# The first norm of a decoder block from the transposed x, by halves of the tokens

## The chip, the cores and the metric

The kernel runs on one core of one Trainium2 chip. A core has a matrix engine (TensorE, PE in the profile; its weight loads are shown apart as PEld), three engines for elementwise work (VectorE or DVE, ScalarE or ACT, GpSimd or POOL), and SyncE (SP), whose queue issues most of the transfers. The transfers of all queues run on the same 16 DMA engines. Each engine works through its own instructions in order and waits on semaphores for the others. The metric is the device time of one execution in microseconds (us).

## The reference

One block of a decoder on x of 1024 tokens by 1024 features, in float32, with a conditioning vector c:

```python
mod = jax.nn.silu(c) @ w_ada[l] + b_ada[l]
sh1, sc1, g1, sh2, sc2, g2 = jnp.split(mod, 6, axis=-1)
h = modulate(rms_norm(x, norm1_g[l]), sh1, sc1)
x = x + g1[:, None, :] * token_mixer(h, w_in[l], ...)
h = modulate(rms_norm(x, norm2_g[l]), sh2, sc2)
x = x + g2[:, None, :] * squared_relu_mlp(h, w_ff1[l], w_ff2[l])
...
return rms_norm(x, norm_f_g)
```

`rms_norm` divides each token by the root of the mean of its squares and multiplies by a gain; `modulate(h, shift, scale)` is h (1 + scale) + shift, with one shift and one scale per feature. The token mixer begins with projections of h by `w_in`; the first that the kernel computes is that of the values of one attention head group (`w_av`). Only the first norm, the first modulation and this first projection matter here.

## The kernel before

Features lie on the 128 partitions, tokens along the free dimension: the transposed x is eight tiles `xt[k]` of 128 features by 1024 tokens, and h is kept as a high part `hh[k]` and a low part `hl[k]`, whose sum has nearly float32's precision. Likewise each weight tile is split into a high part (a cast on ScalarE) and a low part (a subtraction on VectorE), and a product is three matmuls: high by high, low by high, high by low.

`startup` (L392) is the head of the program, written out in order by hand. It issues the loads on SP: c, then x by tokens (eight tiles `xn`, with small tables between them), then for each k the two rows of tiles of `w_ada` that make the scale and the shift of feature slice k (`early_load`, L349) and `xt[k]`, with the first weights (`issue`, L77) in between. Buffers of the size of such a tile come from one pool of 26.

c is spread over all partitions by a matmul with a row of ones, and silu of it is kept in `cb` (L417). ScalarE squares the tiles `xn` and adds up each row as it goes (L419), so that `ss1` holds the sums of squares of all tokens, tokens on partitions. `rstd_of` (L367) makes the reciprocal root: one VectorE instruction, then a power of -1/2 on GpSimd. `rstd_bcast` (L373) spreads the result over all partitions, tokens along the free dimension, by matmuls with an identity; 512 tokens make one half.

A scale or a shift of slice k is the product of silu(c) with 128 columns of `w_ada`. `mod1` (L448) computes it on VectorE: one instruction multiplies a 128 x 1024 tile with `cb` and adds up each row. `h1_mods` (L466) adds the biases and makes the gain `a1`. `h1_scale` (L472) multiplies `xt[k]` by gain and reciprocal root on VectorE, and ScalarE adds the shift and writes `hh[k]`. `h1_low` (L480) writes `hl[k]` on VectorE.

The projection is computed slice by slice of h: `av_first` (L867) has one step for two slices. For slice k its body first prepares slice k+1 (biases, scaling, the low half of a weight if one is due, `hl`, the modulation of slice k+2) and then `av_k` (L840) issues 24 matmuls of 512 columns on slice k, three for each of eight blocks of 128 tokens, which add up in eight PSUM banks. Step 0 starts in `startup`, where slice 0 is scaled by halves. `split_first` (L858) casts a weight tile and puts its low half on a list, `first["lows"]`, from which the bodies take it.

What follows (the other projections, retention, attention, the MLP) is the same in both kernels.

Of the kernel before, what the change touches and what calls it, by code (L numbers as in the profile page):

```python
# [17 lines left out]
P = 128  # L18
# [4 lines left out]
C = 128  # L23
# [110 lines left out]
def block_kernel(ctx, tc, io, stop=None, dbg=None):  # L134
# [214 lines left out]
    def early_load(k):  # L349

        for i in (SC1 + k, SH1 + k):
            early[i] = x4(f"em{i}")
            nc.sync.dma_start(early[i], io["w_ada"][i])
        nc.sync.dma_start(xt[k], io["xT"][k])
# [30 lines left out]
    ss1 = xpool.tile([P, NK], F32, name="ss1")  # L385
# [6 lines left out]
    def startup(issue, prepare, limits):  # L392
# [7 lines left out]
        xn = [x4(f"xn{b}") for b in range(NC)]  # L400
        for b in range(NC):
            nc.sync.dma_start(xn[b], io["x"][b])
            if b == 1:
                nc.sync.dma_start(rel[:32], io["rel_bias"])
                for g in range(3):
                    nc.sync.dma_start(bias_cut(onehot, g)[:33], io["onehot"][:, 384 * g:384 * g + 384])
            if b == 4:
                nc.sync.dma_start(ct, io["cst"])
                nc.sync.dma_start(vec, io["vec"])
# [8 lines left out]
        for b in range(NC):  # L418
            nc.scalar.activation(xn[b], xn[b], AF.Square, accum_out=ss1[:, b:b + 1])  # L419
# [12 lines left out]
        first["lows"].pop(0)()  # L432
        mod1(1, (SH1,))

    def bias_rows(g):

        ps = ps_s(f"pb{g}")[:12, :384]
        nc.tensor.matmul(ps, rel[:33], bias_cut(onehot, g)[:33], start=True, stop=True)
        r = bias_cut(rows, g)[:12]
        nc.scalar.copy(r, ps)  # L440
# [25 lines left out]
    def h1_mods(k):  # L466
        sh = mods[:, SH1 + k:SH1 + k + 1]
        nc.vector.tensor_add(sh, sh, vec[:, VC_BADA + SH1 + k:VC_BADA + SH1 + k + 1])
        nc.vector.scalar_tensor_tensor(a1[:, k:k + 1], mods[:, SC1 + k:SC1 + k + 1], bs1[:, k:k + 1],
                                       vec[:, VC_N1 + k:VC_N1 + k + 1], op0=ALU.add, op1=ALU.mult)  # L470

    def h1_scale(k, j=None):  # L472

        ts = slice(0, S) if j is None else slice(512 * j, 512 * j + 512)
# [5 lines left out]
    def h1_low(k):  # L480
        nc.vector.scalar_tensor_tensor(hl[k], xt[k], mods[:, SH1 + k:SH1 + k + 1], fv(hh[k]),
# [352 lines left out]
    def av_k(g, k, w):  # L834

        ws = slice((k % 2) * 512, (k % 2) * 512 + 512)
        if k == 0:
            av[g] = [ps_s(f"av{g}{c}") for c in range(NC)]
        if g == 0:

            parts = ((hh, 0), (hl, 0), (hh, 1)) if k == 0 else ((hh, 1), (hh, 0), (hl, 0))
            groups = (parts[:1], parts[1:2], parts[2:]) if k == 0 else (parts[:2], parts[2:])
        else:
            parts = ((hh, 1), (hh, 0), (hl, 0))
            groups = (parts,)
        for group in groups:
            for c in range(NC):
                for x, j in group:
                    nc.tensor.matmul(av[g][c], x[k][:, c * C:(c + 1) * C], w[j][:, ws], start=k == 0 and (x, j) == parts[0],
# [7 lines left out]

    def split_first(raw):  # L858
        hi = whl.tile([P, 1024], F32R, tag="wh", name=raw.name + "h")
        lo = whl.tile([P, 1024], F32R, tag="wl", name=raw.name + "l")  # L860
        nc.scalar.copy(hi, raw)
        first["lows"].append(lambda: nc.vector.tensor_sub(lo, raw, fv(hi)))
# [1840 lines left out]
```

## Time and profile before

| | us |
|---|---|
| median of 3 runs | 2194.77 (2193.68 to 2197.47) |
| time of the profiled execution | 2196.09 |
| its span | 2194.1 |
| TensorE busy | 2151.7 (98%) |
| VectorE busy | 1472.7 (67%) |
| ScalarE busy | 944.5 (43%) |
| first matmul of the first projection | 23.14 after the span's start |

The profile is one execution. Its span runs from the first instruction to the last; the time of the same execution is 2.0 us longer. In rows of single instructions the first number is the start in us, the second the duration, then come the engine, the line of the code, the operation, output and inputs by the program's names with their shapes, and in brackets how long the engine had been idle before it and what ended that. TensorE's records overlap: a matmul of 512 columns has a duration of 0.39 us, and the next one starts 0.22 to 0.23 us after it, so spacing counts and not duration.

### The profile page before, as it was taken

The numbers are of one execution on the slowest core, as the hardware profiler recorded it, in microseconds if no ns is written. First come the engines' busy times: TensorE is split into PE (matmuls) and PEld (weight loads), VectorE is DVE, ScalarE is ACT, GpSimd is POOL, SyncE is SP. The second block draws the span as 40 slices with busy tenths as digits, with TensorE's granted clock in tenths as the row PEclk, the third lists the DMA queues.
The fourth block names the chain that finished last, engine by engine and source line by source line (L and its number), as shares of the span: only waits on it lengthen the run. The fifth ranks groups of instructions, "written<-read, shape, count | busy, mean of one in ns | idle before, by whom it ended". The sixth has DMA issues, their size and how long they took to land.

```text
span 2194.1 us, 26997 instructions
## 1 busy us (share of the span) xinstructions
PE 2151.7 (98%) x10034; PEld 1784.1 (81%) x10034; DVE 1472.7 (67%) x2271; ACT 944.5 (43%) x1709; POOL 166.4 (8%) x176
## 2 busy tenths in 40 slices
PE   7999999999999999999999999999999999999998
PEld 5888888888888888888788788888878888788887
DVE  6756777767566677755555644777876665787855
ACT  4532322333334566654544524434454544533412
POOL 0101111100001233200000000001000000000003
PEclk9999999999999999999999999999999999999999
DMA  9869999734687745579523364654154435645322
GB/s 382 227 199 293 289 308 279 222 130 149 244 294 291 250 159 192 173 239 258 151 78 107 106 240 170 234 187 139 44 206 149 152 137 193 243 135 175 113 86 78
DMA packets 159906, 422.54 MB, mean 193 GB/s; under 512 B 27478, under 2 KB 55389, under 8 KB 155358
## 3 DMA queue, kind: packets, MB, share of 16 engines
q1 hardware_dynamic: 151902, 372.57, 48.2%
q0 software_dynamic: 7872, 48.24, 9.5%
q8 instruction: 79, 1.29, 0.2%
q14 instruction: 53, 0.43, 0.1%
HBM read 325.71 MB, written 160.32 MB: 222 GB/s over the span
## 4 chain that ended last, share of the span: by engine, by line
PE 84%; DVE 7%; ACT 4%; DMA 3%; issue 1%; SPq 0%; POOL 0%; POOLq 0%; DVEq 0%; ACTq 0%
PE qap L200 6%; PE qap L204 6%; PE qap L202 6%; PE fp L200 4%; PE fp L202 4%; PE fp L204 4%; PE f2a L202 2%; PE f2a L204 2%; PE f2a L200 2%; PE ak L200 1%; PE ak L202 1%; PE ak L204 1%; PE rg L202 1%; PE rg L200 1%; PE rg L204 1%; PE va L204 1%
## 5 line engine op out<-in xcount | busy, mean ns | idle before, releaser
L200 PE MATMUL qap<-hh,qaw 128*128 128x512 f32 x264 | 102.9, 390 | 0.5 <-DVE qat L291 0.5
L204 PE MATMUL qap<-hh,qaw 128*128 128x512 f32 x264 | 102.7, 389 | 0.0
L202 PE MATMUL qap<-hl,qaw 128*128 128x512 f32 x264 | 102.7, 389 | 0.0
L639 POOL TENSOR_TENSOR j<-qk,j 128x512 fp32r<-128x512 f32 x32 | 48.1, 1506 | 324.1 <-ACT j L638 324.1
L2158 ACT ACTIVATE a<-a 128x512 f32<-128x512 f32 x48 | 30.3, 632 | 78.2 <-DVE a L2157 78.2
L2054 POOL TENSOR_TENSOR accnf<-accnf,sqnf 128x256 f32<-128x256 f32 (+1 forms) x18 | 16.6, 922 | 612.4 <-ACT sqnf L2053 612.4
L1510 ACT ACTIVATE P<-P,ng 128x128 f32<-128x128 f32 (+1 forms) x96 | 41.9, 438 | 43.9 <-DVE ng L1507 43.9
L200 PEld LDWEIGHTS qap<-hh,qaw 128*128 128x128 f32 x264 | 49.5, 188 | 11.5 <-DVE qat L291 1.4
L204 PEld LDWEIGHTS qap<-hh,qaw 128*128 128x128 f32 x264 | 49.6, 188 | 10.3
L202 PEld LDWEIGHTS qap<-hl,qaw 128*128 128x128 f32 x264 | 49.5, 188 | 10.3
L2347 ACT CAST w2h<-w2s 128x512 fp32r<-128x512 f32 x36 | 22.4, 621 | 78.4 <-DVE w2s L2385 78.4
L257 DVE TENSOR_TENSOR fw<-w1r,fw 128x512 fp32r<-128x512 f32 x48 | 32.8, 688 | 33.3 <-ACT fw L247 33.3
L257 DVE TENSOR_TENSOR qaw<-wa,qaw 128x512 fp32r<-128x512 f32 x66 | 45.0, 686 | 12.7 <-ACT qaw L247 12.6
L2054 POOL TENSOR_TENSOR accn<-accn,sqn 128x512 f32<-128x512 f32 x12 | 15.5, 1295 | 477.2 <-ACT sqn L2053 477.2
L247 ACT CAST qaw<-wa 128x512 fp32r<-128x512 f32 x66 | 39.8, 617 | 25.5 <-PE qap L204 15.3
L200 PE MATMUL fp<-h2h,fw 128*128 128x512 f32 x128 | 50.0, 391 | 0.0
L204 PE MATMUL fp<-h2h,fw 128*128 128x512 f32 x128 | 49.8, 389 | 0.0
L202 PE MATMUL fp<-h2l,fw 128*128 128x512 f32 x128 | 49.8, 389 | 0.0
L200 PE MATMUL roa<-rh,rwl 128*128 128x512 f32 x128 | 49.8, 389 | 0.0
L202 PE MATMUL roa<-rl,rwh 128*128 128x512 f32 x128 | 49.8, 389 | 0.0
L204 PE MATMUL roa<-rh,rwh 128*128 128x512 f32 x128 | 49.8, 389 | 0.0
L1288 DVE SCALAR_TENSOR_TENSOR cossin<-cossin,cb 128x1024 f32<-128x1024 f32 x32 | 39.0, 1219 | 15.9 <-DMA cossin<-in_w_ada_dram 15.9
(3057 smaller groups left out, 7106.1 us busy)
## 6 DMA issues: line engine op xcount, KB each, us to landing
cossin<-in_w_ada_dram SPq DMA_DIRECT2D x32, 512.0 KB, 5.4
v<-vd SPq DMA_DIRECT2D x32, 512.0 KB, 4.7
w1r<-in_w_ff_dram SPq DMA_DIRECT2D x32, 512.0 KB, 4.9
vd<-vo SPq DMA_DIRECT2D x24, 512.0 KB, 6.6
yt<-y POOLq DMA_DIRECT2D x6, 2048.0 KB, 15.3
xsd<-as SPq DMA_DIRECT2D x24, 512.0 KB, 3.0
w2r<-in_w_ff2s_dram SPq DMA_DIRECT2D x24, 512.0 KB, 7.4
em<-in_w_ada_dram SPq DMA_DIRECT2D x16, 512.0 KB, 10.2
```

The source lines that it names most:

```text
L200: nc.tensor.matmul(o, wl, xh, start=first, stop=False, skip_group_check=skip)
L202: nc.tensor.matmul(o, wh, xl, start=False, stop=False, skip_group_check=skip)
L204: nc.tensor.matmul(o, wh, xh, start=False, stop=last, skip_group_check=skip)
L247: nc.scalar.copy(t[:, :512], src)
L257: nc.vector.tensor_sub(t[:, 512:], src, fv(t[:, :512]))
L639: nc.gpsimd.tensor_sub(t[:, 1], src, fv(t[:, 0]))
L1288: nc.vector.scalar_tensor_tensor(t, t, 1.0, cb, op0=ALU.mult, op1=ALU.mult, accum_out=mods[:, j:j + 1])
L1510: nc.scalar.activation(v, v, AF.Exp, bias=ng[:, blk:blk + 1], accum_out=st[:, g, blk, 2 + a:3 + a])
L2054: (nc.vector if f == 7 else nc.gpsimd).tensor_add(G["acc", key], G["acc", key], sq)
L2158: nc.scalar.activation(o, o, AF.Relu)
L2347: nc.scalar.copy(hi, src)
```

## The change

x by tokens is no longer loaded, nor is `xn` kept. The transposed x is loaded by halves of 512 tokens: after c, the small tables and the scale tile of slice 0, first the eight first halves, then the shift tile of slice 0 and the first weights, then the eight second halves. The tiles of `w_ada` of the slices 1 to 7 follow.

The sums of squares come from the transposed x. For each half, ScalarE squares the eight tiles (`x_square`), VectorE adds them in pairs, and for each pair TensorE takes 128 tokens at a time as weights against a column of ones (`x_sum`), so that the sums of 128 features and of all pairs add up in PSUM, tokens on partitions. Reciprocal root and broadcast are made for each half by itself. One call of the power on GpSimd on other data is put early.

Scale and shift of slice 1 are computed by TensorE (`mod_rows`): eight accumulating matmuls for each, with a 128 x 128 block of the tile as weights and a column of silu(c) as the moving operand. For that the two tiles are stored in another order on the host, and c is loaded once more by columns (`ccol`). One VectorE instruction copies the two resulting columns from PSUM to `mods`.

Slice 0 is worked through by halves of the tokens in `av_start`: three groups of four matmuls for the first half, with the sums of the second half between them, then `mod_rows` and the second broadcast, then the second half. Its weight is split in halves too. The body of slice 0 then scales slice 1, casts the next weight and takes the second low half; the lower half of that next weight is taken one slice later than before.

```diff
-        nc.sync.dma_start(xt[k], io["xT"][k])
+    def xt_load(k, j):
+        hs = slice(512 * j, 512 * j + 512)
+        nc.sync.dma_start(xt[k][:, hs], io["xT"][k][:, hs])
...
-        xn = [x4(f"xn{b}") for b in range(NC)]
-        for b in range(NC):
-            nc.sync.dma_start(xn[b], io["x"][b])
...
-        for k in range(NK):
-            early_load(k)
-            if k in (0, 1, 3):
-                issue((k + 3) // 2)
+        for t, src in ((ccol, "ccol"), (ct, "cst"), (vec, "vec"), (rel[:32], "rel_bias")):
+            nc.sync.dma_start(t, io[src])
+        for g in range(3):
+            nc.sync.dma_start(bias_cut(onehot, g)[:33], io["onehot"][:, 384 * g:384 * g + 384])
+        first["sq"] = [x4(f"n1sq{i}") for i in range(NK // 2)]
+        early_load(0, (SC1,))
+        for k in range(NK):
+            xt_load(k, 0)
+        early_load(0, (SH1,))
+        issue(1)
+        for k in range(NK):
+            xt_load(k, 1)
...
-        for b in range(NC):
-            nc.scalar.activation(xn[b], xn[b], AF.Square, accum_out=ss1[:, b:b + 1])
-        for g in range(3):
-            bias_rows(g)
-        rs = rstd_of(ss1, "n1", xpool)
-        mod1(0)
+        nc.scalar.activation(ccol, ccol, AF.Silu)
+        mod1(0, (SC1,))
+        pb = [ps_s(f"pb{g}")[:12, :384] for g in range(3)]
+        for g in range(3):
+            nc.tensor.matmul(pb[g], rel[:33], bias_cut(onehot, g)[:33], start=True, stop=True)
+        warm = xpool.tile([P, NK], F32, name="warm")
+        nc.gpsimd.tensor_tensor(warm, ones.to_broadcast([P, NK]), mhalf, op=ALU.pow)
+        for k in range(NK):
+            x_square(k, 0)
+            if k % 2:
+                x_sum(k // 2, 0)
         nc.vector.tensor_scalar_add(bs1, vec[:, VC_BADA + SC1:VC_BADA + SC1 + NK], 1.0)
-        h1_mods(0)
-        first["rb"] = [rstd_bcast(rs, 4 * j, 4, f"n1{j}") for j in range(2)]
+        h1_a(0)
+        rs = rstd_of(first["ss", 0], "n1", xpool)
+        for g in range(3):
+            nc.scalar.copy(bias_cut(rows, g)[:12], pb[g])
         prepare(1)
-        for j in range(2):
-            h1_scale(0, j)
-        mod1(1, (SC1,))
-        h1_low(0)
-        first["lows"].pop(0)()
-        mod1(1, (SH1,))
+        first["rb"] = [rstd_bcast(rs, 0, 4, "n10")]
+        mod1(0, (SH1,))
+        h1_sh(0)
+        for k in range(4):
+            x_square(k, 1)
+        h1_scale(0, 0)
+        x_sum(0, 1)
+        h1_low(0, 0)
+        for k in range(1, NK):
+            early_load(k)
+            if k in (2, 4):
+                issue(k // 2 + 1)
+
+    def x_square(k, j):
+        nc.scalar.activation(first["sq"][k // 2][:, 512 * (k % 2):512 * (k % 2) + 512],
+                             xt[k][:, 512 * j:512 * j + 512], AF.Square)
+
+    def x_sum(i, j):
+        t = first["sq"][i]
+        nc.vector.tensor_add(t[:, :512], t[:, :512], t[:, 512:])
+        if i == 0:
+            first["ss", j] = ps_s(f"n1{j}ss")[:, :4]
+        for b in range(4):
+            nc.tensor.matmul(first["ss", j][:, b:b + 1], t[:, b * P:b * P + P], ones, start=i == b == 0,
+                             stop=i == NK // 2 - 1, skip_group_check=True)
+
+    def mod_rows(i, col):
+        for j in range(NK):
+            nc.tensor.matmul(first["md"][:, col:col + 1], early[i][:, j * P:j * P + P], ccol[:, j:j + 1],
+                             start=j == 0, stop=j == NK - 1)
...
         if k == 0:
-            av[g] = [ps_s(f"av{g}{c}") for c in range(NC)]
...
+            return av_start(g, w)
...
+    def av_start(g, w):
+        av[g] = []
...
+        part(0, hh, 0)
+        for k in range(4, NK):
+            x_square(k, 1)
+        x_sum(1, 1)
+        part(0, hl, 0)
+        first["lows"].pop(0)()
+        x_sum(2, 1)
+        part(0, hh, 1)
+        x_sum(3, 1)
+        rs = rstd_of(first["ss", 1], "n1", xpool)
+        first["md"] = ps_s("md")
+        mod_rows(SC1 + 1, 1)
+        first["rb"].append(rstd_bcast(rs, 0, 4, "n11"))
+        mod_rows(SH1 + 1, 0)
+        for j, rb in enumerate(first["rb"]):
+            nc.scalar.copy(rb1[:, 512 * j:512 * j + 512], rb)
+        h1_scale(0, 1)
+        nc.vector.tensor_copy(mods[:, SH1:SH1 + 2 * NK].rearrange("p (a b) -> p a b", b=NK)[:, :, 1], first["md"][:, :2])
+        h1_mods(1)
+        h1_low(0, 1)
+        for x, j in ((hh, 0), (hl, 0), (hh, 1)):
+            part(1, x, j)
...
                 if k == 0:
-                    for j, rb in enumerate(first["rb"]):
-                        nc.scalar.copy(rb1[:, 512 * j:512 * j + 512], rb)
-                if k % 2 == 0:
+                    av_k(0, k, w)
+                elif k % 2 == 0:
                     ahead(1)
                 if k + 1 < NK:
-                    h1_mods(k + 1)
+                    if k > 0:
+                        h1_mods(k + 1)
                     h1_scale(k + 1)
+                    if k == 0:
+                        ahead(1)
...
-                av_k(0, k, w)
+                if k > 0:
+                    av_k(0, k, w)
```

`part(half, x, j)` issues four matmuls, one for each of four blocks of 128 tokens of that half, with part x of slice 0 as weights and part j of `w_av`'s tile as the moving operand.

More of the change, by code (lines that the diff above doesn't have):

```diff
@@ L837, in av_k @@
         if k == 0:
[L838 to L846 removed]
+            return av_start(g, w)
+        parts = ((hh, 1), (hh, 0), (hl, 0))
+        for group in (parts[:2], parts[2:]):
             for c in range(NC):
                 for x, j in group:
[L849 removed]
+                    nc.tensor.matmul(av[g][c], x[k][:, c * C:(c + 1) * C], w[j][:, ws], start=False,
                                      stop=k == NK - 1 and (x, j) == parts[2], skip_group_check=True)
@@ L860, in split_first @@
         lo = whl.tile([P, 1024], F32R, tag="wl", name=raw.name + "l")
-        nc.scalar.copy(hi, raw)
-        first["lows"].append(lambda: nc.vector.tensor_sub(lo, raw, fv(hi)))
+        for j in (None,) if "split" in first else (0, 1):
+            ts = half(j)
+            nc.scalar.copy(hi[:, ts], raw[:, ts])
+            first["lows"].append(lambda ts=ts: nc.vector.tensor_sub(lo[:, ts], raw[:, ts], fv(hi[:, ts])))
+        first["split"] = True
         return hi, lo
```

46 lines of the change are left out of this document (26 added, 20 removed).

## The prediction

> **What bounds the kernel now.** I read the page first, then the busy time by stretches, then the instructions in order of time for the first 45 us, then single lines of the code. The page has TensorE (PE) busy for nearly the whole span:
>
> ```profile
> span 2194.1 us, 26997 instructions
> PE 2151.7 (98%) x10034; PEld 1784.1 (81%) x10034; DVE 1472.7 (67%) x2271; ACT 944.5 (43%) x1709; POOL 166.4 (8%) x176
> ```
>
> So only a stretch in which TensorE has gaps can be worth anything. In the view by stretches (columns: length, then busy us of PE, PEld, DVE, ACT and POOL with counts, then clock, DMA share, GB/s) the gaps lie at the front, and the last two rows split the run at 61.5 us:
>
> ```profile
> 14.00:23.10 9.10, 3.62 (x16) 3.49 (x16) 3.66 (x9) 5.27 (x9) 2.59 (x1) 1.00 1.03 411
> 31.60:38.00 6.40, 5.77 (x24) 4.42 (x24) 6.27 (x10) 1.17 (x2) 0.00 (x0) 1.00 1.03 410
> 45.00:51.00 6.00, 5.44 (x24) 4.20 (x23) 5.86 (x11) 1.15 (x1) 0.00 (x0) 1.00 1.03 410
> 57.00:63.00 6.00, 5.48 (x25) 4.21 (x23) 5.86 (x11) 1.15 (x1) 1.08 (x1) 1.00 1.07 339
> 61.50:2194.10 2132.60, 2105.02 (x9864) 1751.78 (x9864) 1431.52 (x2205) 918.70 (x1673) 162.23 (x170) 1.00 0.57 187
> ```
>
> Before 23.1 us TensorE has done almost nothing that counts. From 31.6 to 63 us VectorE (DVE) is busy for 5.86 of 6.00 us while TensorE has small gaps: there VectorE prepares one of the eight slices of h after the other, and TensorE follows. After 61.5 us TensorE is busy 2105.0 of 2132.6 us, so a delay of the slices goes one to one into the end. The question is when slice 3 can be scaled, since from there the two kernels run the same instructions. Before, the scalings of slices 1, 2 and 3 start at 29.08, 35.51 and 40.80:
>
> ```profile
> 29.08 1.28 DVE L476 SCALAR_TENSOR_TENSOR xt<-xt,a,rb 128x1024 f32<-128x1024 f32 x1
> 30.28 1.22 DVE L862 TENSOR_TENSOR raw_308l<-raw,raw_308h 128x1024 fp32r<-128x1024 f32 x1
> 31.58 1.28 DVE L481 SCALAR_TENSOR_TENSOR hl<-xt,mods,hh 128x1024 fp32r<-128x1024 f32 x1
> 35.51 1.29 DVE L476 SCALAR_TENSOR_TENSOR xt<-xt,a,rb 128x1024 f32<-128x1024 f32 x1
> 40.80 1.29 DVE L476 SCALAR_TENSOR_TENSOR xt<-xt,a,rb 128x1024 f32<-128x1024 f32 x1
> ```
>
> The first step is longer (6.43 us) than the second (5.29 us), because it holds one lower half of a weight (L862) that the second has not.
>
> The start before the change is one chain. The last square of x by tokens (ACT L419) starts at 15.40, then DVE, POOL (the power -1/2), the broadcast on TensorE, the scaling, the first slice's high part, the first matmul at 23.14:
>
> ```profile
> 15.40 1.06 ACT L419 ACTIVATE xn<-xn 128x1024 f32<-128x1024 f32 x1
> 16.58 0.17 DVE L370 TENSOR_SCALAR n1rs<-ss 128x8 f32<-128x8 f32 x1 [15.48 <-ACT xn L419]
> 16.84 2.59 POOL L371 TENSOR_TENSOR n1rs<-n1rs,ct 128x8 f32<-128x8 f32 x1 [16.39 <-DVE n1rs L370]
> 19.48 2.08 PE L378 MATMUL n10rb<-ct,n1rs 128*128 128x128 f32 x8 [8.38 <-POOL n1rs L371]
> 21.59 0.75 DVE L476 SCALAR_TENSOR_TENSOR xt<-xt,a,n10rb 128x512 f32<-128x512 f32 x1 [2.04 <-PE n10rb L378]
> 22.37 0.72 ACT L478 ACTIVATE hh<-xt,mods 128x512 fp32r<-128x512 f32 x1 [0.79 <-DVE xt L476]
> 23.14 1.35 PEld L849 LDWEIGHTS av<-raw_301h,hh 128*128 128x128 f32 x4 [0.18 <-ACT hh L478]
> 26.43 1.69 PEld L849 LDWEIGHTS av<-raw_301h,hl 128*128 128x128 f32 x8 [0.44 <-DVE hl L481]
> 28.17 1.77 PEld L849 LDWEIGHTS av<-raw_301l,hh 128*128 128x128 f32 x8
> ```
>
> **The change part by part. Loads.** Loads of 512 KB follow each other every 1.28 us: the SP rows of three loads are 3.84 us apart,
>
> ```profile
> 0.74 0.35 SPq L398 DMA_DIRECT2D crow<-in_c_dram  x1
> 1.15 0.83 SPq L402 DMA_DIRECT2D xn<-in_x_dram  x2
> 11.15 1.06 ACT L419 ACTIVATE xn<-xn 128x1024 f32<-128x1024 f32 x1 [0.16 <-DMA xn<-in_x_dram]
> 19.25 0.33 SPq L354 DMA_DIRECT2D xt<-in_xT_dram  x1
> 23.09 0.33 SPq L354 DMA_DIRECT2D xt<-in_xT_dram  x1
> ```
>
> and x by tokens was eight of them, 10.2 us of the queue, which the change drops. It then puts eight small issues ahead of the first big load, at about 0.41 us each on SP (two take 0.83), so the first modulation load is issued at 0.74 + 8 x 0.41 = 4.0. Behind it come eight halves of 256 KB, estimated at half of 1.28. Five loads' worth needs 6.4 us at full pace plus some 2 us from issue to landing: 12.4. Before, the fifth x load, issued with four others from 1.15 on and small ones between, was there at 11.15, ten us later; that pace would give 14.0. I take 12.8, nearer to the first, since the small loads are out of the way by then. The second halves follow behind two more loads of 512 KB and are all there by about 12.8 + 2 x 1.28 + 8 x 0.64 = 20.5. The modulation loads of slice 1 follow by 23.1, the later ones ahead of need; buffers come free early enough, so I cost SP's new order at nothing: what hides it is that no step below waits for a load after 20.5. Without that cover each late load costs up to 1.28.
>
> **Squares and sums of the first half.** ACT's square of 512 elements (0.63) keeps pace with a half. VectorE adds pairs in 0.68 (a 512-wide add). Then four one-column matmuls per pair on TensorE. Nothing at the start shows those, but the last norm's sums have the same form, 128 columns of weights against one column, and the broadcast exists at both speeds (columns of these rows: least/median/most ns, first and last start):
>
> ```profile
> 1505.66 0.63 ACT L2053 ACTIVATE sqn<-x 128x512 f32<-128x512 f32 x1 [0.70 <-DVE x L2079]
> 1502.42 0.68 DVE L242 TENSOR_TENSOR fs<-w1r 128x512 f32<-128x512 f32 x1
> L362 PEld LDWEIGHTS nf0ss<-ct,accnf x8: 192/192/192, 2160.6 to 2161.4; 128*128 128x128 f32 x8
> L362 PE MATMUL nf0ss<-ct,accnf x8: 168/250/250, 2160.7 to 2161.4; 128*128 128x1 f32 x8
> L371 POOL TENSOR_TENSOR n1rs<-n1rs,ct x1: 2587/2587/2587, 16.8 to 16.8; 128x8 f32<-128x8 f32 x1
> L371 POOL TENSOR_TENSOR n20rs<-n20rs,ct x1: 1041/1041/1041, 1511.3 to 1511.3; 128x4 f32<-128x4 f32 x1
> L378 PEld LDWEIGHTS n10rb<-ct,n1rs x8: 287/333/333, 19.5 to 20.9; 128*128 128x128 f32 x8
> L378 PEld LDWEIGHTS n20rb<-ct,n20rs x8: 188/190/192, 1514.5 to 1515.4; 128*128 128x128 f32 x8
> ```
>
> Four calls are eight instruction pairs. Late in the run the eight weight loads start within 0.8 us (2160.6 to 2161.4), 0.115 apart, so one sum holds the queue for 8 x 0.115 = 0.92, which I take as 0.95; a result is there 0.25 after its matmul started. At the start a weight load takes 333 ns instead of 190 and the broadcast's eight are 0.207 apart, though the granted-clock column says 1.00: TensorE is slow there, and a sum is 8 x 0.207 = 1.66 us. The first four matmuls of slice 0 were still slow (1.35 us of weight loads for 4), the eight at 26.43 were not (groups of eight at 26.43 and 28.17: 1.74 us, 0.22 each, so 0.43 at half speed). So TensorE got up to speed some 5 to 6 us after it became busy at 19.48. Two earlier busy stretches did not bring it up to speed:
>
> ```profile
> 2.29 3.75 PE L416 MATMUL pc<-crow,orow 1*128 1x512 f32 x4 [2.29 <-DMA crow<-in_c_dram]
> 7.10 4.00 PE L438 MATMUL pb<-onehot,rel 33*12 33x384 f32 x6 [1.07 <-DMA onehot<-in_onehot_dram]
> ```
>
> The six matmuls of 384 columns take 0.67 each, as three times 0.207 would give. [...]
>
> At slow speed the four sums queue behind the bias matmuls, which end at about 10.0 (6.04 + 4.00): 10.0 + 4 x 1.66 = 16.7, later than the data allow (12.8 + 0.63 + 0.68 + 1.66 = 15.8). Then 0.42 to and through VectorE's row, POOL 1.04 instead of 2.59 (four columns, and a first call has been made earlier, which I take to hold the extra 0.9), the broadcast 2.1 for one half: 17.1, 18.3, 20.4. VectorE scales (0.75) to 21.15 against 22.3 before. The first half thus gains about 1.2 us.
>
> **The second half, on TensorE's queue.** Here the order of instructions decides. VectorE's first add of the second half (0.69) ends at 21.85. TensorE then has, in this order and with nothing that overtakes: sum 0, four matmuls of part hh, sum 1, four of hl, sum 2, four of the low weight, sum 3, eight calls (16 pairs) for one modulation column, the broadcast, 16 pairs for the other. Slow until about 27: sum 1.66 (23.5), four matmuls at 0.43 (25.3), sum 1.66 (26.9). Fast after that: 0.92 + 0.95 + 0.92 + 0.95 (30.65), 16 x 0.115 = 1.85 (32.5), the broadcast 1.1 (33.6), 1.85 (35.5), and 0.25 for the last result: 35.75. POOL's second power lies under the first 16 pairs. VectorE's and ACT's own work here (3 adds, two low parts, four squares) fits beside it and ends near 25.
>
> **What waits behind.** Three VectorE rows of slice 1, one of its two modulation products and the two one-column rows on its sums:
>
> ```profile
> 27.44 1.22 DVE L453 SCALAR_TENSOR_TENSOR em<-em,cb 128x1024 f32<-128x1024 f32 x1
> 28.70 0.16 DVE L468 TENSOR_TENSOR mods<-mods,vec 128x1 f32<-128x1 f32 x1
> 28.77 0.21 DVE L469 SCALAR_TENSOR_TENSOR a<-mods,bs,vec 128x1 f32<-128x1 f32 x1
> ```
>
> VectorE's copy of the two modulation columns waits for the last of them, and behind it in VectorE's queue stand the modulation sums of slice 1, the low part of slice 0's second half and the scaling of slice 1: 0.12 for the copy (estimated by the one-column rows, which follow each other in 0.08 to 0.1), 0.28 for the two one-column rows, 0.05, and 0.75 as the half-width row at 21.59 has it, 1.2 us. So slice 1 is scaled at 36.95 instead of 29.08, 7.9 us later. VectorE no longer multiplies slice 1's two modulation rows (2 x 1.22 us saved), but it saves them inside a wait, which is worth nothing. Besides, the low half of weight 1 slides behind slice 2, so both steps up to slice 3 cost 6.43: 12.86 against 11.72, 1.14 more. Sum: 7.9 + 1.1 = 9.0 us, all of it past slice 3 and carried to the end. The rest (table of c by columns, the host's other order of two rows, the copies of the bias rows, wider use of halves) lies on engines with room: ACT is busy 5.3 of 9.1 us at its fullest there; uncovered, it would be under 1 us.
>
> This sum is made on the profiled execution, whose own time is 2196.09; the median is 2194.77. I add the 9.0 to the median: 2203.8. A difference of 0.2% (4.4 us) is about what can be told from none.
>
> **Rivals.** *Full speed early.* The changed TensorE stream runs almost without a gap from 2.3 to 17 us (4 + 4 us of bias and c, then the sums). If one-column matmuls count as work, TensorE is fast from some 9 to 14 us on. Then: sum 3 ends at 15.05, broadcast 17.85, scaling 18.65, add 19.3; queue of 4 x 0.95 + 3 x 0.92 + 1.85 + 1.1 + 1.85 = 11.4 to 30.65; slice 1 at 32.1; 3.0 + 1.1 = 4.1 us, 2198.9. For it: the gapless stream. Against: the two busy stretches above, which left it slow. [...]
>
> *Slow throughout.* If a stream that is half one-column matmuls does not count, TensorE stays slow until the second part of slice 0: from 25.3, the queue is 3 x 1.66 + 2 x 1.7 + 3.3 + 1.66 + 3.3 = 16.6, to 41.9; slice 1 at 43.4; 14.3 + 1.1 = 15.4 us, 2210.2. For it: 0.207 us per pair is already the row nearest in time. Against: the release at about 25 before.
>
> *Not slower.* One-column calls cost half of the last norm's rows (their pair spacing could there be that of neighbours), and the clock is up early: the queue then waits for VectorE's adds, sums end near 23.7, broadcast 26.3, slice 1 at 28.7: 0.8 us, 2195.5. It decides from a scaling of slice 1 before 32.3. For a real gain that scaling must come before 23.7, which the loads forbid: the first half alone cannot be scaled before 17. Loads that end 10 us sooner would speed up slices 2 to 7 only if these waited for loads; the VectorE rows show no such wait.
>
> **How the numbers follow.** Mixed speed as summed 0.42; full speed early 0.25; slow throughout 0.22; not slower 0.06; loads later than 14 us at mixed speed 0.05 (some 2 us more). Likeliest: 2203.8, by itself 2201 to 2207 (load bounds and the moment of the speed-up). The range runs from just under the full-speed case to the slow one, 2198.3 to 2210.5, and leaves out about 1 in 10 at each end. The full-speed case sits on the 0.2% line, so its chance is split: slower 0.42 + 0.22 + 0.05 + 0.09 = 0.78, within 0.2% 0.16 and a little of the last rival, 0.18, faster 0.04.
>
> **What would show it.** Right: the first matmul of slice 0 about a microsecond or two earlier than 23.14 at best; one-column rows on TensorE of 0.115 to 0.21 us each; a wait of some 8 to 10 us of VectorE's copy for the last modulation column; scaling of slice 3 near 49.8; everything behind it shifted by the same. Wrong: slice 1 scaled before 32, a VectorE wait for loads in slices 1 to 7, or a TensorE gap after 65 us that moves.

## The result and the profile after

The changed kernel takes 2214.51 us (median of 4 runs, 2212.86 to 2217.28); the kernel before, on the same chip, 2195.01. The ratio is 1.0089 with a 95% interval of 1.0071 to 1.0106: 0.9% or 19.5 us slower, in the forecast direction, at more than twice the forecast size (9.0) and outside the range (2198.3 to 2210.5). The profiled execution is the slowest of the four, 2217.28 us.

The page after, and its view by stretches (columns as before):

```profile
span 2215.2 us, 27206 instructions
PE 2176.4 (98%) x10130; PEld 1808.7 (82%) x10130; DVE 1475.9 (67%) x2279; ACT 945.5 (43%) x1711; POOL 168.4 (8%) x178
```

```profile
0.00:61.50 61.50, 54.21 (x197) 43.34 (x198) 27.55 (x48) 22.11 (x34) 6.16 (x8) 1.00 0.81 291
80.00:2215.00 2135.00, 2104.97 (x9862) 1751.77 (x9860) 1430.31 (x2205) 918.98 (x1673) 158.54 (x167) 1.00 0.57 186
```

The bulk has not changed: from 80 us on TensorE is busy for 2105.0 us, as it was after 61.5 us before (2105.02). What grew is the front. VectorE is busy for 27.55 us in the first 61.5 us, and TensorE for 54.21. It is busy but late: the scalings on VectorE, in order of time, and the rows between the last modulation column and slice 1:

```profile
22.32 0.75 DVE L514 SCALAR_TENSOR_TENSOR xt<-xt,a,n10rb 128x512 f32<-128x512 f32 x1 [2.83 <-PE n10rb L382]
41.82 0.75 DVE L514 SCALAR_TENSOR_TENSOR xt<-xt,a,n11rb 128x512 f32<-128x512 f32 x1 [5.78 <-ACT rb L917]
44.41 0.16 DVE L919 COPY mods<-md 128x2 f32<-128x2 f32 x1 [1.84 <-PE md L468]
45.47 1.28 DVE L514 SCALAR_TENSOR_TENSOR xt<-xt,a,rb 128x1024 f32<-128x1024 f32 x1
51.90 1.28 DVE L514 SCALAR_TENSOR_TENSOR xt<-xt,a,rb 128x1024 f32<-128x1024 f32 x1
58.34 1.28 DVE L514 SCALAR_TENSOR_TENSOR xt<-xt,a,rb 128x1024 f32<-128x1024 f32 x1
```

The first half of slice 0 is scaled at 22.32 (21.59 before), slice 1 at 45.47 (29.08), slice 3 at 58.34 (40.80): 17.5 us later. The first matmul of the next stage, qap, starts at 166.78 and started at 149.23, again 17.55 later, so the front's delay is carried on. TensorE's instructions in order of time show how the 23 us between the two scalings were used:

```profile
5.97 4.01 PE L424 MATMUL pb<-onehot,rel 33*12 33x384 f32 x6
10.97 6.98 PE L462 MATMUL n10ss<-ct,n1sq 128*128 128x1 f32 x32 [0.99 <-DVE n1sq L458]
20.21 2.07 PE L382 MATMUL n10rb<-ct,n1rs 128*128 128x128 f32 x8 [2.26 <-POOL n1rs L375]
23.73 1.87 PE L462 MATMUL n11ss<-ct,n1sq 128*128 128x1 f32 x8 [1.44 <-DVE n1sq L458]
25.46 2.05 PE L899 MATMUL av<-raw_297h,hh 128*128 128x512 f32 x4
27.31 1.70 PE L462 MATMUL n11ss<-ct,n1sq 128*128 128x1 f32 x8
28.87 2.05 PE L899 MATMUL av<-raw_297h,hl 128*128 128x512 f32 x4
30.72 1.70 PE L462 MATMUL n11ss<-ct,n1sq 128*128 128x1 f32 x8
32.28 2.05 PE L899 MATMUL av<-raw_297l,hh 128*128 128x512 f32 x4
34.14 1.70 PE L462 MATMUL n11ss<-ct,n1sq 128*128 128x1 f32 x8
35.70 3.55 PE L468 MATMUL md<-ccol,em 128*128 128x1 f32 x16
39.11 2.05 PE L382 MATMUL n11rb<-ct,n1rs 128*128 128x128 f32 x8
40.96 3.41 PE L468 MATMUL md<-ccol,em 128*128 128x1 f32 x16
```

From 23.73 on no row names a wait: TensorE works through its queue without a gap. The order is the one in the prediction. But the rows for 16 one-column pairs take 3.41 to 3.55 us, where 1.85 had been forecast. The weight loads of single tiles (least/median/most ns, first and last start) say why:

```profile
L462 PEld LDWEIGHTS n11ss<-ct,n1sq x32: 288/333/338, 23.7 to 35.4; 128*128 128x128 f32 x32
L468 PEld LDWEIGHTS md<-ccol,em x32: 333/333/333, 35.6 to 43.9; 128*128 128x128 f32 x32
L899 PEld LDWEIGHTS av<-raw_297l,hh x8: 330/330/333, 32.2 to 48.6; 128*128 128x128 f32 x8
```

333 ns is the half-speed value of the prediction (190 is the fast one). TensorE stays at half speed from its start to about 48.6 us, the last 25 us of it gapless work. The clock column says 1.00 all the while, but it is no witness here: the trace records the granted clock only from its first change on (49.4 us in this trace, 24.4 in the one before), and the column counts the time ahead of that as full speed. In e1_wide below it shows half speed.

### The profile page after: what moved, and what is told of

It is laid out like the page before. It is cut to its first block, busy times and chain, and to the rows that moved or that the text cites. A ratio compares the mean times of both kernels' runs of the same rounds, so it can differ in the third digit from the quotient of the medians.

```text
span 2215.2 us, 27206 instructions
## 1 busy us (share of the span) xinstructions
PE 2176.4 (98%) x10130; PEld 1808.7 (82%) x10130; DVE 1475.9 (67%) x2279; ACT 945.5 (43%) x1711; POOL 168.4 (8%) x178
## 4 chain that ended last, share of the span: by engine, by line
PE 84%; DVE 7%; ACT 4%; DMA 3%; issue 1%; SPq 0%; POOL 0%; POOLq 0%; DVEq 0%; ACTq 0%
PE qap L200 6%; PE qap L204 6%; PE qap L202 6%; PE fp L202 4%; PE fp L200 4%; PE fp L204 4%; PE f2a L202 2%; PE f2a L204 2%; PE f2a L200 2%; PE ak L200 1%; PE ak L202 1%; PE ak L204 1%; PE rg L200 1%; PE rg L202 1%; PE rg L204 1%
## 5 line engine op out<-in xcount | busy, mean ns | idle before, releaser
L2127 POOL TENSOR_TENSOR accnf<-accnf,sqnf 128x256 f32<-128x256 f32 (+1 forms) x18 | 16.6, 921 | 611.9 <-ACT sqnf L2126 611.9
L1583 ACT ACTIVATE P<-P,ng 128x128 f32<-128x128 f32 (+1 forms) x96 | 41.9, 438 | 43.4 <-DVE ng L1580 43.4
L247 ACT CAST qaw<-wa 128x512 fp32r<-128x512 f32 x66 | 39.7, 617 | 25.1 <-PE qap L204 15.4
L1965 DVE TENSOR_TENSOR rwl<-rwl,rwh 128x1024 fp32r<-128x1024 f32 x25 | 30.2, 1221 | 29.0 <-ACT rwh L1995 29.0
```

The source lines that it names most:

```text
L247: nc.scalar.copy(t[:, :512], src)
L1583: nc.scalar.activation(v, v, AF.Exp, bias=ng[:, blk:blk + 1], accum_out=st[:, g, blk, 2 + a:3 + a])
L1965: nc.vector.tensor_sub(lo, fv(lo), fv(hi))
L2127: (nc.vector if f == 7 else nc.gpsimd).tensor_add(G["acc", key], G["acc", key], sq)
```

## The experiments

The theory after the result: a stream of one-column matmuls, though gapless, does not bring TensorE up to speed, and the half speed makes the queue of the second half some 9 to 10 us longer than it need be. Rivals: the modulation columns as such are too dear, the sums are too many, or the new order costs this much at any speed. One run answers each; ratios and intervals are against the kernel before on the same chip.

| run | slice 1 scaled | slice 3 scaled | later than before | median | before | ratio (95%) |
|---|---|---|---|---|---|---|
| after | 45.47 | 58.34 | 17.5 | 2214.51 | 2195.01 | 1.0089 (1.0071 to 1.0106) |
| e1_wide | 37.13 | 50.00 | 9.2 | 2204.88 | 2196.76 | 1.0035 (1.0022 to 1.0049) |
| e6_wide32 | 45.70 | 58.56 | 17.8 | 2214.58 | 2196.33 | 1.0084 (1.0071 to 1.0097) |
| e2_modv | 41.93 | 54.81 | 14.0 | 2210.26 | 2196.76 | 1.0065 (1.0046 to 1.0084) |
| e3_mod2x | 52.99 | 65.87 | 25.1 | 2223.95 | 2196.76 | 1.0121 (1.0106 to 1.0136) |
| e4_sum1 | 38.45 | 51.33 | 10.5 | 2207.01 | 2196.76 | 1.0044 (1.0029 to 1.0059) |
| e5_both | 37.48 | 50.35 | 9.6 | 2206.95 | 2196.33 | 1.0050 (1.0037 to 1.0063) |
| e9_widefill | 35.51 | 48.37 | 7.6 | 2204.25 | 2196.06 | 1.0041 (1.0027 to 1.0055) |
| e7_order | 39.16 | 50.24 | 9.4 | 2207.82 | 2196.33 | 1.0049 (1.0037 to 1.0061) |
| e8_fill | 33.80 | 45.53 | 4.7 | 2199.50 | 2196.06 | 1.0019 (1.0010 to 1.0028) |
| e10_fill2 | 31.72 | 43.45 | 2.65 | 2199.60 | 2196.25 | 1.0018 (1.0009 to 1.0027) |

"Later" is the start of slice 3's scaling against 40.80. It and the difference of the medians agree within about 2 us in every run.

**e1_wide: the same instructions, 128 columns wide.** The column of ones and the column of c are each repeated 128 times, the extra columns are not read.

```diff
-            nc.tensor.matmul(first["ss", j][:, b:b + 1], t[:, b * P:b * P + P], ones, start=i == b == 0,
+            nc.tensor.matmul(first["ssw"][:, b * P:b * P + P], t[:, b * P:b * P + P], ones.to_broadcast([P, P]), start=i == b == 0,
...
-            nc.tensor.matmul(first["md"][:, col:col + 1], early[i][:, j * P:j * P + P], ccol[:, j:j + 1],
+            nc.tensor.matmul(first["md"][:, col * P:col * P + P], early[i][:, j * P:j * P + P], ccol[:, j:j + 1].to_broadcast([P, P]),
```

> Every one-column matmul of the changed kernel (the sums of squares and the two modulation columns) gets 128 equal columns instead of one, of which one is read; instructions and weight loads are as many as before. Theory A (TensorE stays at half speed because a stream of one-column matmuls does not count as work): the sums of the first half now bring it up to speed some 5 to 6 us after 11, weight loads fall from 333 to 190 ns before the second half's sums, slice 1 is scaled at 32 to 35 instead of 45.5, time 2201 to 2206. Theory B (the low speed has another cause, such as gaps or the early phase): weight loads stay at 333 ns until 45 or later, slice 1 near 45.5, time about 2214.5.

TensorE's rows in order of time, and the weight loads of its modulation columns:

```profile
19.87 2.00 PE L382 MATMUL n10rb<-ct,n1rs 128*128 128x128 f32 x8 [2.26 <-POOL n1rs L375]
23.31 2.08 PE L463 MATMUL n11ss<-ct,n1sq 128*128 128x128 f32 x8 [1.44 <-DVE n1sq L458]
26.86 1.06 PE L463 MATMUL n11ss<-ct,n1sq 128*128 128x128 f32 x8
31.40 1.95 PE L469 MATMUL md<-ccol,em 128*128 128x128 f32 x16
33.18 1.05 PE L382 MATMUL n11rb<-ct,n1rs 128*128 128x128 f32 x8
34.08 1.95 PE L469 MATMUL md<-ccol,em 128*128 128x128 f32 x16
L469 PEld LDWEIGHTS md<-ccol,em x32: 190/191/192, 31.3 to 35.6; 128*128 128x128 f32 x32
```

The view by stretches of the same run, ahead of the clock's first recorded change and after its second:

```profile
11.00:16.50 5.50, 5.49 (x24) 5.20 (x25) 2.38 (x5) 4.26 (x8) 0.00 (x0) 1.00 1.03 402
20.00:26.80 6.80, 5.36 (x20) 4.77 (x21) 4.51 (x7) 3.04 (x6) 0.00 (x0) 0.50 1.03 406
```

With 128 times as many columns in the same instructions slice 3 comes 8.3 us earlier than in the changed kernel, and the median is 8.1 us above the kernel before where the changed one is 19.5. From 26.86 on the rows take 1.06 and 1.95 instead of 1.70 and 3.5. The speed comes 3.5 us after the stream begins at 23.31. Only the width differs, so the width is the cause. The broadcast at 19.87 shows the other direction: the wide sums of the first half had reached 190 ns at their end, and after 2.26 us of idling TensorE is slow again (2.00). The second stretch says what slow is: the granted clock is 0.50 from 20.0 to 26.8, where weight loads take 333 ns (in the first stretch they take 333 too, but the record has not begun). Slice 1 comes at 37.13 and not at the expected 32 to 35: the first half's sums brought the speed up only at their end, at 16.6, and the gap lost it again.

**e6_wide32: 32 columns instead of 128.**

```diff
-            nc.tensor.matmul(first["ss", j][:, b:b + 1], t[:, b * P:b * P + P], ones, start=i == b == 0,
+            nc.tensor.matmul(first["ssw"][:, b * P:b * P + 32], t[:, b * P:b * P + P], ones.to_broadcast([P, 32]), start=i == b == 0,
...
-            nc.tensor.matmul(first["md"][:, col:col + 1], early[i][:, j * P:j * P + P], ccol[:, j:j + 1],
+            nc.tensor.matmul(first["md"][:, col * P:col * P + 32], early[i][:, j * P:j * P + P], ccol[:, j:j + 1].to_broadcast([P, 32]),
```

> As the run with 128 equal columns, but with 32: where between one and 128 columns does the stream count as work? If what counts is the share of time in which columns stream, and 32 of 128 are too few, TensorE stays at half speed: slice 1 near 45.5, time 2214.5. If a few columns are enough: slice 1 near 37, time near 2205. I hold the first for likelier, 6 to 4.

```profile
L463 PEld LDWEIGHTS n11ss<-ct,n1sq x32: 286/333/333, 23.9 to 35.6; 128*128 128x128 f32 x32
L469 PEld LDWEIGHTS md<-ccol,em x32: 333/333/333, 35.8 to 44.1; 128*128 128x128 f32 x32
```

Slow throughout, 2214.58: for this mix 32 columns are too few and 128 enough. Where between them it turns was not run.

**e4_sum1: one set of sums per half.** VectorE adds the pairs up first, and TensorE sums once.

```diff
+        else:
+            s = first["sq"][0]
+            nc.vector.tensor_add(s[:, :512], s[:, :512], t[:, :512])
+            t = s
-        for b in range(4):
-            nc.tensor.matmul(first["ss", j][:, b:b + 1], t[:, b * P:b * P + P], ones, start=i == b == 0,
+        for b in range(4) if i == NK // 2 - 1 else ():
+            nc.tensor.matmul(first["ss", j][:, b:b + 1], t[:, b * P:b * P + P], ones, start=b == 0,
```

> The changed kernel with the four pair sums of a half added up by VectorE (three more adds of 0.68 us a half) and only one set of four one-column calls on TensorE for each half instead of four sets. If TensorE's queue between the two broadcasts sets slice 1: three sums of 1.7 us leave it, of which some 0.4 us return as VectorE's adds, slice 1 near 41, time near 2210. If VectorE's own work were what sets it: up to 2 us later, 2216.5.

```profile
24.08 2.08 PE L903 MATMUL av<-raw_297h,hh 128*128 128x512 f32 x4 [1.60 <-ACT hh L520]
27.66 1.62 PE L903 MATMUL av<-raw_297l,hh 128*128 128x512 f32 x4
29.45 1.05 PE L466 MATMUL n11ss<-ct,n1sq 128*128 128x1 f32 x8 [0.17 <-DVE n1sq L463]
30.37 1.93 PE L472 MATMUL md<-ccol,em 128*128 128x1 f32 x16
32.15 2.00 PE L382 MATMUL n11rb<-ct,n1rs 128*128 128x128 f32 x8
33.94 3.41 PE L472 MATMUL md<-ccol,em 128*128 128x1 f32 x16
```

Both directions stand in one trace. The three groups of 512 columns, now without one-column sums between them, bring TensorE up: the sum takes 1.05 and the first modulation column 1.93. After these 2.7 us of one-column work, with no gap, the broadcast takes 2.00 and the second column 3.41: TensorE is slow again. So the one-column stream did not only fail to raise the speed, as in the changed kernel: here 2.7 us of it lost it. (The granted clock is 1.00 from 28.8 to 32.2 and 0.50 from there to 42.5.) That the speed would come up at all was not in the expectation, and slice 1 is scaled at 38.45 instead of near 41.

**e2_modv: the modulation of slice 1 on VectorE as before**, TensorE's columns and the copy gone, the rest as changed.

```diff
+        mod1(1)
         rs = rstd_of(first["ss", 1], "n1", xpool)
-        first["md"] = ps_s("md")
-        mod_rows(SC1 + 1, 1)
+        nc.vector.memset(ps_s("md")[:, :2], 0.0)
         first["rb"].append(rstd_bcast(rs, 0, 4, "n11"))
-        mod_rows(SH1 + 1, 0)
...
-        nc.vector.tensor_copy(mods[:, SH1:SH1 + 2 * NK].rearrange("p (a b) -> p a b", b=NK)[:, :, 1], first["md"][:, :2])
```

> The changed kernel with the modulation of slice 1 back on VectorE (two products of 128 x 1024, put behind the last pair sum of the second half), so 32 one-column matmul pairs less. If VectorE's wait for the second modulation column is what sets slice 1: the second broadcast starts when GpSimd's power is done, near 37.2 instead of 39.1, no copy waits behind it, slice 1 is scaled near 42 instead of 45.5, time near 2211. If TensorE's queue ahead of it or the loads set slice 1: no change, 2214.5.

Slice 1 at 41.93, 3.5 us earlier than in the changed kernel, for some 6.7 us taken out of TensorE's queue: with the columns gone, the power (35.93 to 36.94) and ACT's copy of the broadcast (39.10 to 39.69) lie bare. The dear columns are part of the loss, not the whole.

**e3_mod2x: the modulation columns computed twice**, the second set not read.

```diff
+        for j in range(NK):
+            nc.tensor.matmul(first["md"][:, 2 + col:3 + col], early[i][:, j * P:j * P + P], ccol[:, j:j + 1],
+                             start=j == 0, stop=j == NK - 1, skip_group_check=True)
```

> The changed kernel with the 32 matmul pairs of the two modulation columns issued twice (the second set into columns that nobody reads). It measures the disputed price by itself. At half speed and on the path: 7 us later, slice 1 near 52.5, time near 2221.5. At the full-speed price of the prediction (0.115 us a pair): 3.7 us, 2218. Off the path: 2214.5.

Slice 1 at 52.99, 7.5 us later, of which 0.7 was there already at slice 0. The other 6.8 over 32 more pairs are 0.21 each: TensorE's queue sets the end one to one, and a pair costs its half-speed price.

**e5_both: e4 and e2 together**, with the modulation of slice 1 behind the row that feeds GpSimd's second power.

> The changed kernel with both earlier edits: one set of one-column calls for each half, and the modulation of slice 1 on VectorE, now behind the row that feeds GpSimd's second power. Theory A (one-column streams keep TensorE at half speed or bring it back there): the twelve matmuls of part one bring TensorE up to speed by about 29 and nothing takes it back; sum at full speed, power some 1.9 us beside VectorE's products, broadcast 1.2 us, slice 1 scaled at 36 to 37, time 2203 to 2206. Theory B (speed has another cause): broadcast at 2.1 us, slice 1 later than 37.5.

```profile
29.34 1.38 PE L466 MATMUL n11ss<-ct,n1sq 128*128 128x1 f32 x8
32.97 1.65 PE L382 MATMUL n11rb<-ct,n1rs 128*128 128x128 f32 x8 [2.25 <-POOL n1rs L375]
36.83 2.08 PE L903 MATMUL av<-raw_297h,hh 128*128 128x512 f32 x4 [2.21 <-ACT hh L520]
L382 PEld LDWEIGHTS n11rb<-ct,n1rs x8: 185/230/338, 33.0 to 34.0; 128*128 128x128 f32 x8
```

The speed comes up inside the sum (1.38, between 1.05 and 1.87). With nothing left in TensorE's queue it then idles 2.25 us for GpSimd, and loses the speed inside the broadcast: the first weight loads take 185 to 190 ns, the last ones 333 to 338 (the granted clock falls at 33.5). After 2.21 more us of waiting for ACT's high part it is still slow. So theory A is right that the twelve matmuls bring TensorE up, and wrong that nothing takes it back: the gap does. Slice 1 comes at 37.48, 1 us earlier than in e4 and just behind the expected 36 to 37: the chain of the second half itself (sum, power, broadcast, copy, scaling) now sets it, and that chain is there at any speed.

**e9_widefill: e1, and fill meant to make TensorE fast from the beginning.** Matmuls of 512 columns, whose result is not read, fill the gaps ahead of the bias matmuls, the power and the first scaling.

```diff
+        nc.vector.memset(rb1[:, :512], 1.0)
+        fill(1)
...
+        fill(3)
         pb = [ps_s(f"pb{g}")[:12, :384] for g in range(3)]
...
+        fill(2)
         rs = rstd_of(first["ss", 0], "n1", xpool)
...
+        fill(1)
         mod1(0, (SH1,))
```

> The run with 128 equal columns, and in addition the same kind of fill on TensorE in its idle time from the start (one call ahead of the first matmul, three ahead of the bias matmuls, two ahead of the first broadcast, one behind it). This is the prediction's rival of full speed from early on, made true. If its sum holds: sums of 0.95 us, the first broadcast at full speed, slice 1 scaled at 32 to 33.5 instead of 37.1, time about 4 us above before, 2200 to 2202. If something other than TensorE's speed sets slice 1: 37 as in the run without fill, 2205.

```profile
7.40 5.25 PE L418 MATMUL fill<-rb 128*128 128x512 f32 x6
12.59 2.10 PE L432 MATMUL pb<-onehot,rel 33*12 33x384 f32 x6
14.62 3.84 PE L473 MATMUL n10ss<-ct,n1sq 128*128 128x128 f32 x32
20.72 1.16 PE L382 MATMUL n10rb<-ct,n1rs 128*128 128x128 f32 x8 [0.54 <-POOL n1rs L375]
29.77 1.95 PE L479 MATMUL md<-ccol,em 128*128 128x128 f32 x16
32.45 1.95 PE L479 MATMUL md<-ccol,em 128*128 128x128 f32 x16
```

The fill ahead of the bias matmuls is itself still slow (0.88 us for each of the six, against 0.47 for each of the four at 18.30); the granted clock rises at 12.3, and from 12.59 on everything up to slice 1 runs at full speed. The change still costs 7.6 us at slice 3 and 8.2 us in the median, and slice 1 at 35.51 misses the expected 32 to 33.5. The fill has a price of its own in this: it holds the first half's sums until 18.46, where their last addition (14.83 + 0.69) and 0.95 for a sum would allow about 16.5. So the order alone costs between some 5.6 us (estimated, with those 2 us given back) and 7.6.

**e7_order: a version meant to beat both.** x's halves loaded first, one set of sums, slice 1's modulation on VectorE, the second half's first sums ahead of slice 0's matmuls, the bias matmuls moved behind.

```diff
         for k in range(NK):
             xt_load(k, 0)
+        for t, src in ((ct, "cst"), (vec, "vec"), (rel[:32], "rel_bias")):
+            nc.sync.dma_start(t, io[src])
...
+        bias_rows(0)
         for k in range(4):
             x_square(k, 1)
+            if k % 2:
+                x_sum(k // 2, 1)
```

> A version meant to beat both kernels: no load of x by tokens, squares by halves with one set of one-column calls for each half, all modulation on VectorE, first halves of x loaded ahead of everything but c, the modulation of slice 1 and the low halves of the first two weights done while the second half's sums are on their way, slice 1 scaled ahead of the low part of slice 0's second half. If the order on VectorE and TensorE is what costs: slice 1 scaled at 26 to 27 and slice 3 near 38 instead of 40.8, 2 to 3 us less than before, near 2192.5. If the loads or TensorE's half speed hold the second broadcast: slice 3 at 39 to 41, the time of before. GpSimd's first power runs with VectorE idle and its second beside a VectorE product: if that is why the same power took 1.92 and 1.01 us, they take about 1.0 and 1.9.

It ends at 2207.82. The expectation missed by 15 us. TensorE was slow here too (up to 47.3), and two bias matmuls (2.7 us at half speed, from 32.98) stood in the queue ahead of the second broadcast, which began at 35.64; the power was done at 33.34. VectorE's own order costs as well: the first half's sums ended at 14.82, but the row on them ran at 17.55, behind two modulation products, and the broadcast ended at 20.93, but the first scaling came at 22.76, behind three additions of the second half. So this run does not show that no order of the work could gain.

**e8_fill and e10_fill2: the kernel before, with unread matmuls to bring TensorE up to speed** ahead of the first broadcast: seven ahead of the power, or five right behind the bias matmuls.

```diff
+        nc.vector.memset(rb1[:, :512], 1.0)
+        fl = ps_s("fill")
...
+        fill(7)
         rs = rstd_of(ss1, "n1", xpool)
```

> The kernel before, with seven matmuls of 512 float32 columns on a tile of ones put into TensorE's idle time ahead of the first broadcast (their result is read by nobody). Theory A (TensorE's speed follows from how densely columns stream): the broadcast's weight loads take 190 instead of 333 ns, the first scaling starts near 20.7 instead of 21.6, everything behind it 0.9 us earlier, which the time can hardly show: 2194 to 2197 beside 2196. Theory B (the start of a program is slow whatever runs): the broadcast stays at 333 ns, and if the fill runs over, the first scaling comes later.

> The kernel before with five matmuls of 512 columns on a tile of ones right behind the bias matmuls, so that they run from about 11 on while TensorE waits for the norm; in the first try they started at 17.3 and ran into the broadcast. If density of columns sets TensorE's speed: the first broadcast's weight loads at 190 ns, slice 0 scaled near 20.7 instead of 21.6 and slice 1 near 28.2 instead of 29.1, time 0.9 us less, which is inside what can be told (2194 to 2197 beside 2196). If the fill is still running at 19.5: later by what it overruns.

VectorE's write of the fill's operand and TensorE's rows in e10_fill2:

```profile
16.34 0.48 DVE L414 MEMSET rb<- 128x512 f32 x1 [15.25 <-ACT xn L421]
16.88 7.23 PE L426 MATMUL fill<-rb 128*128 128x512 f32 x10 [5.96 <-DVE n1rs L370]
23.95 1.05 PE L378 MATMUL n10rb<-ct,n1rs 128*128 128x128 f32 x8
```

The fill did raise the speed (the broadcast takes 1.05 for one half instead of 2.08), but it began only at 16.88 instead of at about 11, and so held the broadcast from 19.48 to 23.95. It began so late because its operand did: VectorE wrote the tile of ones only at 16.34, after waiting for ScalarE's last square of x by tokens (16.73 in e8_fill). The changed kernel has no such squares, and in e9_widefill the same write ran at 1.15. Why it waits for the squares is not shown, and so it stays open what a fill in time would have done. Both versions are about 0.2% slower than the kernel before. No version here beats that one.

## Why the prediction was right or wrong

**Right: the bound and the mechanism.** TensorE's bulk is unchanged (2105 us), loads do not hold the second half, VectorE's copy waits for the last modulation column (in place of one wait of 8 to 10 us VectorE has three: 8.85 for the sums at 35.87, 5.78 at 41.82 and 1.84 at 44.41), and slice 1's scaling stands behind it. From the last column's end at 44.38 to slice 1 it takes 1.09 us, forecast 1.2. The steps from slice 1 to 3 take 12.87, forecast 12.86.

**The step that failed: "Slow until about 27 ... Fast after that".** From the first sum of the second half to the last modulation column the queue took 20.65 us (23.73 to 44.38); forecast 13.9. That is 6.75 of the 8.5 us by which slice 1 came later than said (45.47 against 36.95). The mistake was to date the speed-up from the start of work, "some 5 to 6 us after it became busy at 19.48". The trace before had it with 128- and 512-column matmuls alone in the queue; the same stretch of time with one-column sums between them was taken to count as the same work. Where the columns are widened, slice 1 comes at 37.13 (e1), near the forecast 36.95; in part that is luck, since there the second half's first sum starts 1.5 us late and the queue takes 12.7 us, 1.2 less than forecast. The prediction had asked this very question in two of its rivals, and it gave the case in which one-column calls do not count 0.22.

**The second miss: the first half.** It was scaled at 22.32, forecast 20.4. Working it back: the sums started at 10.97, not 10.0, because the first addition ended then (0.97); four sums took 7.0 rather than 6.64 (0.3); the power took 1.92 instead of 1.04 and the hand-overs around it were 0.2 quicker (0.7); the rest fits. The reason given for 1.04, an earlier first call "which I take to hold the extra 0.9", is wrong: the warm call had been made, at 3.85, and the power still took 1.92. The last section shows what it ran beside.

**The rivals.** *Slow throughout* is what happened. Its queue of 20.05 us (21.85 to 41.9) is 0.6 short of the measured one, and its slice 1 at 43.4 is early by the same 1.9 us of the first half. With that added, it gives 2212. *Full speed early* had 4.1 us; e9 made its condition true and cost 7.6. Its first scaling ended at 22.66 instead of 18.65, 4.0 us late, and the queue and what followed it made up 0.6, which gives the 3.4 us between slice 1 at 35.51 and at 32.1. The late scaling comes from three things: the last addition ended at 15.52 instead of 14.1, the fill held the sums 2 us, and the power took 1.93. No run shows TensorE fast from 9 to 14 us on with one-column sums, as that rival had it: in after the granted clock first rises at 49.4, in e9, with 512-column fill and 128-column sums, at 12.3. By the runs a rise of that kind comes with 512-column and 128-column work (3.5 us after the stream begins in e1, 5.4 in e10) and did not come in after in the 25 us to 48.6, half of them one-column matmuls. *Not slower* did not come near.

**The 17.5 us at slice 3, divided by the runs:** 10 us are half speed (58.34 against 48.37 in e9), 8.3 of which go with the columns' width alone (e1). 7.6 are the order of work, up to 2 of which may be e9's own fill; half speed's share is then larger by as much. The median difference of 19.5 is 2 us more than slice 3's delay. In the profiles, the one after taken in the slowest of its runs, the spans differ by 21.1, 3.5 more than that delay; where this comes from is not shown.

## What to carry to other kernels

Before moving a reduction or a vector product onto TensorE as one-column matmuls, price each at its weight load, at both speeds (here 0.115 and 0.21 us per pair), and ask what it does to the speed of its neighbours. In this start the thin stream went with weight loads of 333 ns until 48.6 us (after), and with the column repeated 128 times the change cost 8.1 us instead of 19.5 (e1). At the start of a program read TensorE's speed from the weight loads of one shape (here 333 and 190 ns): in these traces the clock column shows 0.50 only once its record has begun (at 49.4 us in after).

## What the hardware showed that had not been expected

**Being busy was not enough for full speed.** 25 us without a gap, half of them one-column matmuls, at 333 ns per weight load (after); 128 columns, same instructions, up to speed in 3.5 us (e1); 2.7 us of one-column work enough to lose it (e4); 32 columns no help (e6). And gaps of 2.26 us (e1, at 19.87) and 2.25 us (e5, at 32.97) were enough to lose it.

**The clock changed on a grid of 3.4 us.** In the traces' record of the granted clock the changes of the first 50 us lie 3.41 us or a multiple of it apart: up at 16.6, down at 20.0, up at 26.8 in e1; 28.8, 32.2, 42.5 in e4; 30.1, 33.5, 40.3 in e5. Later in after it is 0.50 for one such stretch, 1131.45 to 1134.87. In before, after, e1 to e5 and e8 to e10 the first rise ends a stretch of 3.4 us in which 128- or 512-column matmuls filled at least three quarters of the time (in after 46.0 to 49.4, in e10 18.9 to 22.3). The stretches ahead of these falls were mostly idle (e1, with TensorE busy 1.04 of 3.30 us, and e5) or mostly one-column work (e4). In the changed kernel's queue one-column sums took half of the time, and there was no rise. That may be why the same kind of stream needed 3.5 us in one run and 5.4 in another, by where in the grid it began; no run varied that alone.

**GpSimd's power took 0.9 us longer beside a VectorE product.** The power's rows in the changed kernel:

```profile
18.23 1.92 POOL L375 TENSOR_TENSOR n1rs<-n1rs,ct 128x4 f32<-128x4 f32 x1 [12.74 <-DVE n1rs L374]
36.11 1.01 POOL L375 TENSOR_TENSOR n1rs<-n1rs,ct 128x4 f32<-128x4 f32 x1 [15.96 <-DVE n1rs L374]
```

and the VectorE row that stood beside the first:

```profile
18.07 1.22 DVE L482 SCALAR_TENSOR_TENSOR em<-em,cb 128x1024 f32<-128x1024 f32 x1
```

The first power ends 0.86 us after VectorE's product does (20.15 against 19.29). In e7 it is the other way round: the first power (17.79, VectorE idle) takes 1.02 and the second (31.41, beside a product from 31.25 to 32.47) 1.93, ending 0.87 after the product. So this power took 1.01 to 1.02 without a VectorE product beside it and 1.92 to 1.93 with one, as far as GpSimd's spans can be trusted; why is not shown. The product was not longer for it: in e5 a second product follows at 31.98 beside the same power (31.00 to 32.92) and takes its usual 1.22. The kernel before has a longer power too: its first power (128x8) ends at 19.43, 1.5 us after the product that began just ahead of it (at 16.69), and takes 2.59, where the warm call of that size takes 1.64 alone. The 0.9 us lies on the path of the first half in the changed kernel.

**VectorE waited for a copy that it did not use.** In e2 the second broadcast ended at 39.06, ACT copied it from 39.10 to 39.69, and VectorE scaled from the same tile only at 39.72 (the changed kernel has the same pause at 41.82, where nothing hangs on it). The copies stand ahead of the scaling in the program. In e7 the scaling stands ahead of the copy: it starts at 37.76, 0.05 us after the broadcast's end at 37.71 and 0.78 ahead of the copy at 38.54. So the order in the program decides it, as far as one run shows.
